# Wider weight blocks, undivided rooms and another last turn in a mixture-of-experts stage

## The chip, the core and the metric

The kernel runs on one core of a Trainium2 chip. The metric is the device time of one execution in microseconds (us). A core has five engines that each work through an own list of instructions: TensorE (PE; the load of a matmul's stationary tile is listed as PEld), VectorE (DVE), ScalarE (ACT), GpSimd (POOL) and SyncE (SP). SP issues nearly all transfers (DMAs) here; sixteen DMA engines that all queues share carry them out.

## The reference

Two layers work on 256 latent and 256 context tokens of width 1024. A layer modulates its input, projects it, runs 8 heads of windowed attention beside 8 heads of a chunked state-space scan (SSD), projects both back and normalises; then a feed-forward part follows, dense in layer 0 and a mixture of experts in layer 1:

```python
def _moe(h, router, wg, wu, wd):
    top_v, top_i = lax.top_k((h @ router).astype(jnp.float32), TOP_K)      # 2 of 8
    gates = jax.nn.softmax(top_v, axis=-1)
    combine = jnp.sum(jax.nn.one_hot(top_i, N_EXPERTS) * gates[..., None], axis=-2)
    for e in range(N_EXPERTS):
        out = out + combine[..., e:e + 1] * _swiglu(h, wg[e], wu[e], wd[e])
```

`_swiglu` is (silu(h Wg) * (h Wu)) Wd with Wg, Wu of 1024 x 3584 and Wd of 3584 x 1024, all float32: 44.04 MB for an expert, 352.3 MB for eight, read once in each execution. Only latent tokens reach the experts.

## The kernel before

**The experts (`jobs`, L1340).** The experts are ranked by how many tokens chose them, and each rank has a fixed number of slots for tokens (32, 64, 96 or 192). Seven turns run in the rank order 0, 4, 2, 3, 5, 7, 6, with 32, 64, 96, 64, 64, 32 and 64 slots. Rank 1, with 192 slots (three tiles of 64), is the side expert, worked off in seven pieces between blocks of the turns. A turn cuts the 3584 hidden columns into blocks (`main`: 1024, 1024, 1024, 512); the side expert's pieces are 512 wide (`thin`). A step of one block loads gate and up weights and multiplies the gathered tokens with them (`gate_up`, in two halves), transposes the hidden values of the step before (`flip`), forms silu(gate)*up (`act`), and multiplies the hidden values of the step before with that block's rows of Wd (`down`). After an expert's last block its result is scattered back to the tokens (`evac`, `scatter`). A matmul has the tokens (64 or 32 columns) as its stationary tile and up to 512 weight columns as the moving one, so a tile of 32 slots costs PE half of what one of 64 costs.

**The rooms.** Every weight transfer of an expert is one call of `moe_raw` (L1268): 1 MB goes into the next of 15 rooms, which are taken in strict rotation and reused when the matmuls on their old contents are done. One row of a block that is contiguous in memory is one packet for each partition: 4 KB for 1024 columns, 2 KB for 512. A tile of Wd takes two neighbouring rows a partition, an 8 KB packet. Five of the 15 rooms are pairs of two 512 KB buffers: one in `accl`, and four made of `whi` and `wlo` of the pool `sp`. Into these a load goes as two transfers, a row of Wd at a time (4 KB packets).

**The pool `sp` earlier.** `whi` and `wlo` have four buffers each. Weight splitting (`split_unit`, L117, which makes a high and a low part of a float32 weight for three matmuls) takes one of both. In the mixers the decay matrices of the scan (`E`, L770: one of 512 KB for each 128 tokens and each of two head groups, read back through SP from `cscr`) take `wlo`, and the transposed attention weights (`pT`, L900) take `whi`.

**The order.** PE's list in the experts' stage is the order of the code. In the mixers attention, scan and the modulation (`wm`, 2 MB loads of w_mod and their matmuls `mod`) are woven together, and a planner places instructions; SP issues in the order in which the planner meets them, and an SP instruction that waits for its room holds all that stand behind it. POOL multiplies E (L775), builds W (L779, L782), the scan's scaled inputs xe (L722) and more, in its own order.

**The end.** The last block of the last turn closes the kernel: `gate_up`, `act`, `flip`, its rows of Wd, `evac`, the scatter straight into four `fin` banks that already hold the residual (`add_acc`), layer norm, and the output.

Of the kernel before, what the change touches and what calls it, by code (L numbers as in the profile page):

```python
# [18 lines left out]
P = 128  # L19
D = 1024  # L20
# [49 lines left out]
class Build:  # L70
# [44 lines left out]
    def split_unit(self, src, shape, nm="u"):  # L115

        nc = self.nc  # L117
        self.uid += 1
        hi = self.sp.tile(shape, F32R, tag="whi", name=f"{nm}h{self.uid}")
        lo = self.sp.tile(shape, F32R, tag="wlo", name=f"{nm}l{self.uid}")  # L120
        with self.tc.issue_after(self.hold.pop(0).ins) if self.hold else ExitStack():
            nc.scalar.activation(hi, src, AF.Copy)  # L122
        self.nsplit += 1
        if self.pool_share and self.nsplit % self.pool_share == 0:
            self.last_pooled = nc.gpsimd.tensor_tensor(lo, src, hi, op=OP.subtract)
        else:
            nc.vector.tensor_tensor(lo, src, hi, op=OP.subtract)  # L127
        return hi, lo
# [371 lines left out]
    def steps_dt(self, l, m, pp, dtt, at, lv):  # L500
# [5 lines left out]
        wd = self.sp.tile([P, NK, 32], F32R, tag="whi", name=f"wd{l}")  # L506
# [207 lines left out]
    def ssd(self, l, wk, lv, dtt, mix, tts):  # L714
# [45 lines left out]
        for tt in tts:  # L760
# [4 lines left out]
            for g in range(2):  # L765
# [4 lines left out]
                E = self.sp.tile([P, 2, 4, P], F32, tag="wlo", name=f"E{l}{tt}{g}")  # L770
# [54 lines left out]
    def attention(self, l, wk, qT, kT, v, mix, tts, q0):  # L825
# [60 lines left out]
        for n in range(len(items) + 1):  # L886
# [56 lines left out]
    def last_norm(self, xs):  # L943
# [3 lines left out]
        out = [self.sp.tile([P, D], F32, tag="whi", name=f"fin{self.uid}{i}") for i in range(2)]  # L947
# [320 lines left out]
    def moe_raw(self, src, nm, paired=False):  # L1268

        self.uid += 1  # L1270
# [4 lines left out]
        if isinstance(pool, list):  # L1275
            halves = []
            for i, (p, tag) in enumerate(pool):
                t = p.tile([P, D], F32, tag=tag, name=f"{nm}{self.uid}{i}").rearrange("p (k f) -> p k f", f=f)
                self.nc.sync.dma_start(t, rows[:, i * n // 2:(i + 1) * n // 2, :])
                halves.append(t)  # L1280
            return halves
        if pool is None:
            self.odd ^= 1
            t = self.first_raw[:, self.odd, :].rearrange("p (k f) -> p k f", f=f)
        else:
            t = pool.tile([P, n, f], F32, tag="mraw", name=f"{nm}{self.uid}")
        self.nc.sync.dma_start(t, rows)
        return [t[:, :n // 2, :], t[:, n // 2:, :]]
# [62 lines left out]
    def jobs(self, M, todo, J0=None, side=None, finish=None):  # L1351
# [7 lines left out]
        main = [(0, 1024), (1024, 1024), (2048, 1024), (3072, 512)]  # L1359
        thin = [(f, 512) for f in range(0, FE, 512)]  # L1360

# [5 lines left out]
        def banks(J, w):  # L1367

            return [[self.bank("gu") for _ in range(w // 512 if s == 64 else 1)] for s in J["tiles"]]

        def gate_up(J, blk, os, part):
            c0, w = blk
            kn = 2048 // w
            for r in range(part * NK // kn // 2, (part + 1) * NK // kn // 2):
                gr, ur = [self.moe_raw(weights(a[n][0], J["e"], r * kn * P, (r + 1) * kn * P, c0, c0 + w), "mg")
                          for n in ("moe_w_gate", "moe_w_up")]
                at = lambda m, kk: m[kk // (kn // 2)][:, kk % (kn // 2), :]
                for q, s in enumerate(J["tiles"]):
                    for kk in range(kn):
                        k = r * kn + kk  # L1380
                        g, u = at(gr, kk), at(ur, kk)
                        x = J["xe"][:, k, q * 64:q * 64 + s]
                        if s == 64:
                            for b, o in enumerate(os[q]):
                                cs = slice(b * 512, (b + 1) * 512)
                                self.beside(o, x, [g[:, cs], u[:, cs]], k == 0, k == NK - 1)
                        else:
                            hs = [slice(b * w // 2, (b + 1) * w // 2) for b in range(2)]
                            self.beside(os[q][0], x, [m[:, h] for m in (g, u) for h in hs], k == 0, k == NK - 1)
                for _ in range(kn):  # L1390
                    self.tick()

        def act(J, blk, os):

            hs, n = [], 0
            for s, two in zip(J["tiles"], os):
                w = 512 if s == 64 else blk[1] // 2
                for o in two:
                    if n % 2 == 0 or w < 512:
                        self.uid += 1  # L1400
                        t = pj.tile([P, 512], F32, tag="h", bufs=2, name=f"h{J['nm']}{self.uid}")
                        hs.append((t, w, []))
                        n = 0
                    h = t[n * 64:n * 64 + 64, :w]
                    nc.scalar.activation(h, o[:64, :w], AF.Silu)  # L1405
                    nc.vector.tensor_tensor(h, h, o[64:, :w], op=OP.mult)  # L1406
                    hs[-1][2].append(n)
                    n += 1
            return hs

        def flip(J, blk, hs):
# [14 lines left out]
            for s in J["tiles"]:  # L1426
                if s == 64:
                    hT = [flipped.pop(0) for _ in range(blk[1] // 512)]
                    out.append(lambda t, odd, hT=hT: hT[t // 2][:, t % 2 * 2 + odd, :])
                else:  # L1430
                    hT, m = flipped.pop(0), blk[1] // 512
                    out.append(lambda t, odd, hT=hT, m=m: hT[:, t % m * 2 + odd, t // m * 32:t // m * 32 + 32])
# [6 lines left out]
        def parts(s, rd):  # L1439
            w = D * s // P  # L1440
            return [rd[:, 0, c:c + w] for c in range(0, D, w)]

        def down(J, c, blk, hT):
            last = c == len(main) - 1
            if J["side"]:
                os = [self.bank("ys") for _ in hT]
            elif c == 0:
                os = J["y"] = [self.bank("y") for _ in hT]
            else:
                os = J["y"]  # L1450
            nt = blk[1] // 256
            for t in range(nt):
                rd = rows(J, blk, t)
                for s, o, x in zip(J["tiles"], os, hT):
                    for odd in range(2):
                        self.beside(o, x(t, odd), parts(s, rd[odd]), t + odd == 0 and (J["side"] or c == 0),
                                    t == nt - 1 and odd == 1 and (J["side"] or last))
            if not J["side"]:
                return
            for y, o in zip(J["ys"], os):  # L1460
                if c == 0:
                    nc.scalar.activation(y, o, AF.Copy)
                else:
                    nc.vector.tensor_tensor(y, y, o, op=OP.add)
# [74 lines left out]
        after = [(0, 1), (0, 2), (3, 3), (4, 3), (5, 0), (5, 2), (6, 0)]  # L1539
        steps = []  # L1540
        for n in range(len(todo)):
            for c in range(len(main)):
                steps.append((n, c))
                if (n, c) in after and side is not None:
                    steps.append(("side", after.index((n, c))))
# [10 lines left out]
        for n, c in steps + [(None, None)]:  # L1556
            if n is not None:
                need(n)
                blk = (thin if n == "side" else main)[c]
# [3 lines left out]
                if todo and (n, c) == (0, 1):  # L1563
                    fill("side", self.slots(J["side"], M, *side, f"s{self.uid}_", True))
                if n == 0 and c == 2:
                    fill("close", M["close"]())
                if n != "side" and c == 2 and n + 1 < len(todo):
                    fill(n + 1, self.slots(J[n + 1], M, *todo[n + 1], f"t{n + 1}_{self.uid}_"))
                os = banks(J[n], blk[1])
# [4 lines left out]
            if n is not None:  # L1574
                gate_up(J[n], blk, os, 1)
# [316 lines left out]
```

## Time and profile before

| | |
|---|---|
| median of 3 runs | 1830.56 us (1828.31 to 1832.91) |
| profiled execution | 1831.6 us, of which the span of its instructions is 1829.8 |
| mean granted clock of PE | 0.973 |
| busy share of the span | PE 95%, DVE 39%, ACT 26%, POOL 11% |
| traffic | 499.27 MB in 176000 packets |
| experts' stage | first weight transfer issued at 914.5 us, first matmul at about 974 us, last matmul of Wd ends at 1812.6 us |

The profile page cuts the span into 40 slices of 45.7 us; a digit is the busy share in tenths. The DMA share is the mean over 16 DMA engines of the time that their packets took; packets of neighbouring transfers overlap a little, so it can stand over 1. An instruction's time in the timeline is a group's first start and the length of the run of that group.

### The profile page before, as it was taken

The page shows a single profiled execution, that of the slowest core. Times are in us where ns is not written, and L with a number is a line of the kernel's source. Part 1 is how long each engine was busy: PE and PEld are TensorE (multiplying, and loading weights), DVE is VectorE, ACT ScalarE, POOL GpSimd, SP SyncE. Part 2 cuts the span into 40 slices and gives each one's busy share as a digit, 9 for nine tenths or more (in the row PEclk, how much of TensorE's full clock was granted, in tenths as well). Part 3 has the DMA queues.
Part 4 walks back from the last instruction along what each step waited for, and adds up shares of the span by engine and source line. Part 5 has one row for each costly group of instructions (what it writes and reads, how often), then busy time and mean ns, then how long its engine had stood idle before and what let it go on. Part 6 is the DMA issues. An engine that isn't in the chain of part 4 may idle for free.

```text
span 1829.8 us, 25533 instructions
## 1 busy us (share of the span) xinstructions
PE 1734.6 (95%) x10236; PEld 1037.4 (57%) x10236; DVE 712.8 (39%) x1232; ACT 476.2 (26%) x856; POOL 203.3 (11%) x202
## 2 busy tenths in 40 slices
PE   6999998999999999999899999999999999989996
PEld 4788446798988899887465343323333343333332
DVE  3356585772443368768675011101021110110122
ACT  1333454353222235545342110101011110000011
POOL 2000650230000041501412000000000000000000
PEclk8999999999999999999998999999999999999998
DMA  9533985131223212254879999999999999999994
GB/s 330 185 128 122 318 282 166 70 115 70 91 93 138 92 51 95 68 193 148 305 293 357 411 412 413 414 414 412 416 418 405 414 411 412 411 411 410 412 410 199
DMA packets 176000, 499.27 MB, mean 273 GB/s; under 512 B 32616, under 2 KB 43424, under 8 KB 161344
## 3 DMA queue, kind: packets, MB, share of 16 engines
q1 hardware_dynamic: 174848, 495.76, 70.7%
q8 instruction: 82, 1.34, 0.3%
q10 hardware_dynamic: 608, 1.58, 0.3%
q0 software_dynamic: 416, 0.21, 0.1%
q14 instruction: 46, 0.38, 0.1%
HBM read 496.37 MB, written 4.30 MB: 274 GB/s over the span
## 4 chain that ended last, share of the span: by engine, by line
PE 84%; DMA 7%; DVE 5%; ACT 1%; POOL 1%; issue 1%; SPq 0%; DVEq 0%; ACTq 0%; POOLq 0%
PE gu L1349 24%; PE y L1349 8%; PE fm L460 7%; PE fm L459 7%; PE fm L461 7%; PE ys L1349 4%; DMA mg<-in_moe_w_up_dram 3%; PE tm L459 3%; PE tm L460 3%; PE tm L461 3%; DMA wm<-in_w_mod_dram 2%; PE fo L461 2%; PE fo L460 2%; PE fo L459 2%; PE xe L1319 2%; PE hT L1419 1%
## 5 line engine op out<-in xcount | busy, mean ns | idle before, releaser
L460 PE MATMUL fm<-mlo,uh 128*128 128x512 f32 (+1 forms) x768 | 265.7, 347 | 8.9 <-DVE mlo L395 8.9
L459 PE MATMUL fm<-mhi,uh 128*128 128x512 f32 (+1 forms) x768 | 265.1, 348 | 6.7 <-ACT uh L122 4.3
L461 PE MATMUL fm<-mhi,ul 128*128 128x512 f32 (+1 forms) x768 | 264.3, 346 | 0.0
L460 PEld LDWEIGHTS fm<-mlo,uh 128*128 128x128 f32 x768 | 147.4, 192 | 29.4 <-DVE mlo L395 12.0
L459 PEld LDWEIGHTS fm<-mhi,uh 128*128 128x128 f32 x768 | 146.6, 192 | 27.0 <-ACT uh L122 4.5
L1406 DVE TENSOR_TENSOR ht<-ht,gu 64x512 f32<-64x512 f32 (+1 forms) x47 | 31.6, 673 | 327.8 <-ACT ht L1405 327.7
L461 PEld LDWEIGHTS fm<-mhi,ul 128*128 128x128 f32 x768 | 147.1, 192 | 18.4 <-DVE ul L127 0.8
L1349 PE MATMUL y<-md,hht 128*32 128x256 f32 (+1 forms) x1048 | 149.4, 495 | 1.7 <-DMA md<-in_moe_w_down_dram 1.7
L1349 PE MATMUL gu<-mg,xes__8731 128*64 128x512 f32 x600 | 141.6, 603 | 2.1 <-DMA mg<-in_moe_w_up_dram 1.2
L931 POOL TENSOR_TENSOR mv<-mv,mhalf 128x1 f32<-128x1 f32 x12 | 8.5, 722 | 941.9 <-DVE mv L930 941.6
L1349 PEld LDWEIGHTS y<-md,hht 128*32 128x32 f32 (+1 forms) x1048 | 50.7, 125 | 99.4 <-issue 82.8
L459 PE MATMUL fo<-uh,hh 128*128 128x256 f32 (+1 forms) x336 | 95.3, 286 | 0.0
L460 PE MATMUL fo<-ul,hh 128*128 128x256 f32 (+1 forms) x336 | 95.0, 285 | 0.0
L1423 ACT ACTIVATE hht<-hT 128x512 f32<-128x512 f32 (+2 forms) x32 | 15.0, 473 | 306.4 <-PE hT L1419 306.4
L1349 PEld LDWEIGHTS gu<-mg,xes__8731 128*64 128x64 f32 x600 | 44.7, 139 | 85.5 <-issue 78.9
L461 PE MATMUL fo<-uh,hl 128*128 128x256 f32 (+1 forms) x336 | 92.5, 285 | 0.0
L1406 DVE TENSOR_TENSOR hs<-hs,gu 64x512 f32<-64x512 f32 x21 | 14.5, 690 | 177.4 <-ACT hs L1405 177.4
L1349 PE MATMUL gu<-mg,xet__9610 128*64 128x512 f32 (+2 forms) x416 | 72.4, 565 | 2.1 <-DMA mg<-in_moe_w_up_dram 1.5
L460 PEld LDWEIGHTS fo<-ul,hh 128*128 128x128 f32 x336 | 63.3, 188 | 0.7
L459 PEld LDWEIGHTS fo<-uh,hh 128*128 128x128 f32 x336 | 63.0, 188 | 0.8
L461 PEld LDWEIGHTS fo<-uh,hl 128*128 128x128 f32 x336 | 62.0, 188 | 0.7
L1349 PE MATMUL ys<-md,hhs 128*64 128x512 f32 x264 | 59.3, 605 | 0.0
(443 smaller groups left out, 2860.4 us busy)
## 6 DMA issues: line engine op xcount, KB each, us to landing
mg<-in_moe_w_up_dram SPq DMA_DIRECT2D x64, 1024.0 KB
mg<-in_moe_w_gate_dram SPq DMA_DIRECT2D x61, 1024.0 KB
md<-in_moe_w_down_dram SPq DMA_DIRECT2D x55, 1024.0 KB
wm<-in_w_mod_dram SPq DMA_DIRECT2D x20, 2048.0 KB
md<-in_moe_w_down_dram SPq DMA_DIRECT2D x78, 512.0 KB
mg<-in_moe_w_gate_dram SPq DMA_DIRECT2D x72, 512.0 KB
mg<-in_moe_w_up_dram SPq DMA_DIRECT2D x70, 512.0 KB
mraw<-in_moe_w_down_dram SPq DMA_DIRECT2D x18, 1024.0 KB
```

The source lines that it names most:

```text
L459: nc.tensor.matmul(ps, ah, bh, start=first and i == 0, stop=False)
L460: nc.tensor.matmul(ps, ah, bl, start=False, stop=False)
L461: nc.tensor.matmul(ps, al, bh, start=False, stop=last and i == n - 1)
L931: self.last_pow = nc.gpsimd.tensor_tensor(mv[:, 2:3], mv[:, 2:3], self.mhalf[:, 0:1], op=OP.pow)
L1319: nc.tensor.matmul(tp[:, m * W:(m + 1) * W], M["xn"][i][:, j * P:(j + 1) * P], pick[i][:, :, 0:W // n], start=(i == 0), stop=(i == 1))
L1349: self.last_mm = self.nc.tensor.matmul(o[n * g:n * g + n, :w.shape[1]], x, w, start=first, stop=last)
L1406: nc.vector.tensor_tensor(h, h, o[64:, :w], op=OP.mult)
L1419: self.last_flip = nc.tensor.transpose(tp[:, jj * m:(jj + 1) * m], h[:m, c0:c0 + 255:2], self.ident[:m, :m])
L1423: nc.scalar.activation(t[:, :k, :m], tp[:, :k * m].rearrange("p (j s) -> p j s", j=k), AF.Copy)
```

## The change

Three things change in the experts, and one in the pool `sp`.

The pool `sp` has one tag `w` with four contiguous buffers of 1 MB in place of `whi` and `wlo`. A split weight takes one (both parts), E takes one for both head groups of 128 tokens, pT one for both heads of a pair. As a room such a buffer is filled by one transfer. The `accl` room stays a pair.

Turns with at most 64 slots run in blocks of 2048 and 1536 columns, a 128-row slice of gate or of up being one transfer (8 KB or 6 KB a partition, 1 MB or 768 KB). The turn of 96 slots and the last turn keep the four old blocks. The rank order becomes 0, 4, 2, 3, 5, 6, 7: the last turn has 32 slots and not 64. The pieces of the side expert stand behind other blocks, two of them in the first and two in the last turn, where there were two and one.

In a step, the late scatter and the preparation of the next expert move ahead of the second half of `gate_up`. The side expert's `down` issues both transfers of Wd rows first. At the end, the `fin` banks are taken after `act` and `flip`.

```diff
@@ split_unit, L117
-        hi = self.sp.tile(shape, F32R, tag="whi", name=f"{nm}h{self.uid}")
-        lo = self.sp.tile(shape, F32R, tag="wlo", name=f"{nm}l{self.uid}")
+        t = self.sp.tile([P, 2, D], F32R, tag="w", name=f"{nm}{self.uid}")
+        hi, lo = [t[:, i, :shape[1] * shape[2]].rearrange("p (a b) -> p a b", a=shape[1]) for i in range(2)]
...
@@ ssd, L770
-                E = self.sp.tile([P, 2, 4, P], F32, tag="wlo", name=f"E{l}{tt}{g}")
+                if g == 0:
+                    E2 = self.sp.tile([P, 2, D], F32, tag="w", name=f"E{l}{tt}")
+                E = E2[:, g].rearrange("p (r h t) -> p r h t", r=2, h=4)
...
@@ attention, L899
-                    if i == 0:
-                        pTs[hh] = self.sp.tile([P, 4, 256], F32, tag="whi", name=f"pT{l}{pair[0]}{h0 + hh}")
+                    if i == 0 and hh == 0:
+                        t = self.sp.tile([P, 2, D], F32, tag="w", name=f"pT{l}{pair[0]}{h0}")
+                        pTs = {n: t[:, n].rearrange("p (k q) -> p k q", k=4) for n in range(2)}
...
@@ moe_raw, L1275
             for i, (p, tag) in enumerate(pool):
-                t = p.tile([P, D], F32, tag=tag, name=f"{nm}{self.uid}{i}").rearrange("p (k f) -> p k f", f=f)
-                self.nc.sync.dma_start(t, rows[:, i * n // 2:(i + 1) * n // 2, :])
+                part = rows[:, i * n // 2:(i + 1) * n // 2, :] if n > 1 else rows[:, :, i * D:min(f, (i + 1) * D)]
...
+        elif isinstance(pool, tuple):
+            t = pool[0].tile([P, 2, D], F32, tag=pool[1], name=f"{nm}{self.uid}").rearrange("p a b -> p (a b)")
...
@@ jobs, L1359
-        main = [(0, 1024), (1024, 1024), (2048, 1024), (3072, 512)]
+
+        wide, mid = [(0, 2048), (2048, 1536)], [(0, 1024), (1024, 1024), (2048, 1024), (3072, 512)]
         thin = [(f, 512) for f in range(0, FE, 512)]
+        turns = [mid if t[2] > 64 or n == 6 else wide for n, t in enumerate(todo)]
+        blocks = lambda n: thin if n == "side" else turns[n]
...
-            kn = 2048 // w
+            kn = max(1, 2048 // w) if w != 1536 else 1
...
@@ down, L1439
             if J["side"]:
-                os = [self.bank("ys") for _ in hT]
...
+                rds = [rows(J, blk, t) for t in range(nt)]
+                for y, s, x in zip(J["ys"], J["tiles"], hT):
+                    o = self.bank("ys")
...
@@ the steps, L1539
-        after = [(0, 1), (0, 2), (3, 3), (4, 3), (5, 0), (5, 2), (6, 0)]
+        after = [(0, 0), (0, 1), (3, 1), (4, 1), (5, 1), (6, 0), (6, 1)]
...
             if prev is not None:
                 pn, pc, pb, h = prev
                 hT = flip(J[pn], pb, h)
+            if late is not None:
+                need("close")
+                scatter(J[late])
+                late = None
             if n is not None:
...
                 gate_up(J[n], blk, os, 1)
                 if finish and (n, c) == steps[-1]:
                     break
                 h = act(J[n], blk, os)
-            if late is not None:
-                need("close")
-                scatter(J[late])
-                late = None
...
@@ the end of jobs, L1594
+        rds = [rows(J, blk, t) for t in range(blk[1] // 256)]
+        h = act(J, blk, os)
+        hT = flip(J, blk, h)[0]
+        s = J["tiles"][0]
         fin = [[self.bank("fin") for _ in range(2)] for _ in range(2)]
...
@@ body, L1836
-                              [(self.sp, "whi"), (self.sp, "wlo")]]
+                              (self.sp, "w")]
...
-                    ranks = [0, 4, 2, 3, 5, 7, 6]
+                    ranks = [0, 4, 2, 3, 5, 6, 7]
                     self.jobs(M, [(turn[t], p, {0: 32, 2: 96, 7: 32}.get(p, 64), bt) for t, p in enumerate(ranks)], J0,
```

What SP issues in the mixer of layer 0, before and after. `wm` are the 2 MB loads of w_mod, `bias` the attention's biases, `wo` the two loads of the output projection's weights.

```order
29 L771 DMA E_1675<-cscr_106 128x2x512
30 L771 DMA E_1747<-cscr_106 128x2x512
31 L771 DMA E_1826<-cscr_106 128x2x512
32 L771 DMA E_1891<-cscr_106 128x2x512
33 L445 DMA bias_1943<-rscr_108 64x6x64 x4
...
47 L771 DMA E_2291<-cscr_106 128x2x512
48 L261 DMA wm_2233<-in_w_mod_dram 128x2x2048
49 L445 DMA bias_2243<-rscr_108 64x6x64 x4
50 L451 DMA wo_2563<-in_w_out_dram 128x8x512
51 L451 DMA wo_2693<-in_w_out_dram 128x8x512
52 L445 DMA bias_2370<-rscr_108 64x6x64 x4
```

```order
29 L445 DMA bias_1913<-rscr_108 64x6x64 x4
...
35 L261 DMA wm_1843<-in_w_mod_dram 128x2x2048
36 L773 DMA E_1649<-cscr_106 128x2x512 x2
37 L261 DMA wm_1873<-in_w_mod_dram 128x2x2048
...
44 L445 DMA bias_2210<-rscr_108 64x6x64 x4
45 L451 DMA wo_2527<-in_w_out_dram 128x8x512
46 L451 DMA wo_2653<-in_w_out_dram 128x8x512
47 L773 DMA E_2179<-cscr_106 128x2x512 x2
48 L445 DMA bias_2335<-rscr_108 64x6x64 x4
```

Four E of two token tiles stood ahead of the biases and of five of the `wm`; the first two now stand behind four more `wm`, and the last two behind both `wo` instead of ahead of them.

What PE does at the end, from the rows of Wd of the last block but one: `y` the products with Wd, `hT` the transposes of `flip`, `fin` the residual's banks.

```order
5922 L1349 MATMUL y_12403<-mraw_8213,hht_1298_1430_12696 64x512 x8
5923 L1349 MATMUL y_12403<-md_12722,hht_1298_1430_12696 64x512 x4
5924 L1349 MATMUL y_12403<-md_12728,hht_1298_1430_12696 64x512 x4
5925 L1419 MATMUL hT_12745<-cA,ht_1298_1443_12742 128x64 x4
5926 L1601 MATMUL fin_12734<-res_2531,cA 128x512
5927 L1601 MATMUL fin_12735<-res_2531,cA 128x512
5928 L1349 MATMUL y_12403<-md_12738,hht_1298_1445_12750 64x512 x4
5929 L1349 MATMUL y_12403<-md_12740,hht_1298_1445_12750 64x512 x4
```

```order
5793 L1361 MATMUL y_11917<-md_12375,hht_1303_1443_12299 32x256 x8
5794 L1361 MATMUL y_11917<-md_12385,hht_1303_1443_12299 32x256 x8
5795 L1361 MATMUL y_11917<-md_12395,hht_1303_1443_12299 32x256 x8
5796 L1438 MATMUL hT_12414<-cA,ht_1303_1456_12411 128x64 x2
5797 L1632 MATMUL fin_12419<-res_2495,cA 128x512
5798 L1632 MATMUL fin_12420<-res_2495,cA 128x512
5799 L1361 MATMUL y_11917<-md_12405,hht_1303_1458_12417 32x256 x4
5800 L1361 MATMUL y_11917<-md_12407,hht_1303_1458_12417 32x256 x4
5801 L1361 MATMUL y_11917<-md_12409,hht_1303_1458_12417 32x256 x8
```

The order at the end is the same; the matmuls have 256 moving columns where they had 512, twice as many of them for a tile of Wd.

## Rows read from the trace of the kernel before

**Rows 1.** The page's 40 slices: PE, DMA and GB/s.

```profile
PE   6999998999999999999899999999999999989996
DMA  9533985131223212254879999999999999999994
GB/s 330 185 128 122 318 282 166 70 115 70 91 93 138 92 51 95 68 193 148 305 293 357 411 412 413 414 414 412 416 418 405 414 411 412 411 411 410 412 410 199
```

**Rows 2.** Busy us (x count) per stretch: PE, PEld, DVE, ACT, POOL; PEclk, DMA share, GB/s.

```profile
1000.00:1200.00 200.00, 192.43 (x1174) 74.74 (x1170) 26.30 (x62) 22.15 (x44) 0.00 (x0) 0.99 1.03 412
1200.00:1400.00 200.00, 195.42 (x1194) 69.80 (x1194) 30.24 (x60) 20.77 (x41) 0.00 (x0) 0.97 1.03 414
1400.00:1600.00 200.00, 196.80 (x974) 70.30 (x974) 26.36 (x45) 19.26 (x36) 0.00 (x0) 0.99 1.03 412
1600.00:1780.00 180.00, 172.65 (x1052) 63.54 (x1044) 26.07 (x43) 17.61 (x34) 0.00 (x0) 0.96 1.03 411
```

**Rows 3.** All transfers of three stretches: 1045 to 1050, 1105 to 1150, 1790 to 1795.

```profile
DMA packets 1033, 1.99 MB, mean 398 GB/s; under 512 B 62, under 2 KB 62, under 8 KB 1033
DMA packets 4893, 18.57 MB, mean 413 GB/s; under 512 B 364, under 2 KB 364, under 8 KB 4891
DMA packets 289, 2.12 MB, mean 424 GB/s; under 512 B 31, under 2 KB 31, under 8 KB 31
```

**Rows 4.** The page's transfers of Wd: count, KB of each.

```profile
md<-in_moe_w_down_dram SPq DMA_DIRECT2D x55, 1024.0 KB
md<-in_moe_w_down_dram SPq DMA_DIRECT2D x78, 512.0 KB
mraw<-in_moe_w_down_dram SPq DMA_DIRECT2D x18, 1024.0 KB
```

**Rows 5.** Transfers of the stretch 1802 to 1806.

```profile
DMA packets 173, 0.69 MB, mean 172 GB/s; under 512 B 23, under 2 KB 23, under 8 KB 155
```

**Rows 6.** Timeline of PE and DVE at the end: start, length, engine, line, operation, count.

```profile
1807.07 1.99 PE L1601 MATMUL fin<-res,cA 128*128 128x512 f32 x4
...
1808.99 3.65 PE L1349 MATMUL y<-md,hht 128*64 128x512 f32 x16
1812.57 1.99 PE L1601 MATMUL fin<-res,cA 128*128 128x512 f32 x4
1812.69 0.75 DVE L1477 SCALAR_TENSOR_TENSOR yst<-y,wst,g 128x512 f32<-128x512 f32 x1 [11.68 <-PE y L1349]
```

**Rows 7.** Timeline of PE in an expert of 32 slots.

```profile
1110.76 1.93 PE L1349 MATMUL y<-mraw,hht 128*32 128x256 f32 x32
```

**Rows 8.** Timeline of DVE after an expert of 32 slots.

```profile
1704.96 1.96 DVE L1482 SCALAR_TENSOR_TENSOR yst<-y,wst,g 32x256 f32<-32x256 f32 x4 [0.55 <-PE y L1349]
```

**Rows 9.** Chain of waits in layer 0's mixer: start, length, what.

```profile
187.92 11.93 DMA wm<-in_w_mod_dram
...
224.75 13.46 DMA wm<-in_w_mod_dram
...
277.05 0.85 PE yd L792 x8
...
285.55 0.62 DVE mix L820 x2
...
297.97 2.07 ACT mxh L986 x4
```

**Rows 10.** Timeline of SP in layer 0's mixer.

```profile
238.34 0.37 SPq L771 DMA_DIRECT2D E<-cscr  x1
...
250.71 16.30 SPq L451 DMA_DIRECT2D wo<-in_w_out_dram  x2
267.10 4.20 SPq L445 DMA_DIRECT2D bias<-rscr  x4
```

**Rows 11.** Timeline of POOL: the last E of layer 0.

```profile
257.81 1.89 POOL L775 TENSOR_TENSOR E<-E,cs 128x1024 f32<-128x1024 f32 x1
```

**Rows 12.** Chain of waits in layer 1's mixer.

```profile
853.29 8.78 DMA E<-cscr
...
869.84 2.04 POOL xe L722 x2
```

**Rows 13.** Timeline of POOL at the first E of layer 1.

```profile
862.21 3.78 POOL L775 TENSOR_TENSOR E<-E,cs 128x1024 f32<-128x1024 f32 x2 [11.50 <-DMA E<-cscr]
```

More of the change, by code (lines that the diff above doesn't have):

```diff
@@ L946, in last_norm @@
         self.uid += 1
-        out = [self.sp.tile([P, D], F32, tag="whi", name=f"fin{self.uid}{i}") for i in range(2)]
+        out = self.sp.tile([P, 2, D], F32, tag="w", name=f"fin{self.uid}")
+        out = [out[:, i] for i in range(2)]
         gl = self.mraw[0].tile([P, 2, D], F32, tag="mraw", name=f"gl{self.uid}")
@@ L1536, in need @@
                 self.tick()
-        after = [(0, 1), (0, 2), (3, 3), (4, 3), (5, 0), (5, 2), (6, 0)]
-        steps = []
+        after = [(0, 0), (0, 1), (3, 1), (4, 1), (5, 1), (6, 0), (6, 1)]
+        steps, ns = [], 0
         for n in range(len(todo)):
-            for c in range(len(main)):
+            for c in range(len(turns[n])):
                 steps.append((n, c))
-                if (n, c) in after and side is not None:
-                    steps.append(("side", after.index((n, c))))
+                for _ in range(after.count((n, c)) if side is not None else 0):
+                    steps.append(("side", ns))
+                    ns += 1
         if not todo:
@@ L1558, in jobs @@
                 need(n)
-                blk = (thin if n == "side" else main)[c]
+                J[n]["blocks"] = blocks(n)
+                blk = blocks(n)[c]
                 if n == "side" and c == 0:
@@ L1562, in jobs @@
                                   for q in range(len(J[n]["tiles"]))]
[L1563 to L1569, printed above, removed]
+                os = banks(J[n], blk)
                 gate_up(J[n], blk, os, 0)
@@ L1573, in jobs @@
                 hT = flip(J[pn], pb, h)
+            if late is not None:
+                need("close")
+                scatter(J[late])
+                late = None
             if n is not None:
+                if todo and (n, c) == (0, 0):
+                    fill("side", self.slots(J["side"], M, *side, f"s{self.uid}_", True))
+                if (n, c) == (0, 1):
+                    fill("close", M["close"]())
+                if n != "side" and c == len(blocks(n)) // 2 and n + 1 < len(todo):
+                    fill(n + 1, self.slots(J[n + 1], M, *todo[n + 1], f"t{n + 1}_{self.uid}_"))
                 gate_up(J[n], blk, os, 1)
@@ L1602, in add_acc @@
                                                     start=True, stop=False)
-        rds = [rows(J, blk, t) for t in range(blk[1] // 256)]
-        h = act(J, blk, os)
-        hT = flip(J, blk, h)[0]
-        s = J["tiles"][0]
         add_acc(0, self.last_flip)
@@ L1610, in jobs @@
             for odd in range(2):
-                self.beside(J["y"][0], hT(t, odd), parts(s, rd[odd]), False, t == len(rds) - 1 and odd == 1)
+                self.beside(J["y"][0], hT[t][odd], parts(s, rd, odd), False, t == len(rds) - 1 and odd == 1)
         add_acc(1, self.last_mm)
```

128 lines of the change are left out of this document (70 added, 58 removed).

## The prediction

> **What bounds the kernel now.** I read the page's slices first, then busy time by stretch, then the transfers of chosen stretches, then the end's timeline and the chain of waits in the two mixers.
>
> The slices fall into two parts [rows 1]: up to about 960 us PE is busy and the DMA engines mostly are not; from about 1000 to 1780 us both are, and the rate stays between 405 and 418 GB/s. The stretches decide between the two [rows 2]: from 1000 to 1780 us the DMA share is 1.03 in each, while PE adds up to 192.43 + 195.42 + 196.80 + 172.65 = 757.3 of 780 us. PE has 22.7 us of idle time left and the transfers none: the experts' stage is bound by transfers, with PE close behind. How fast a byte comes therefore sets the length of that stage, how far PE is behind at its end sets the rest, and what happens before 914 us shifts the start.
>
> **Packets: what removing them is worth.** Three stretches are each almost of one packet size [rows 3]. Without the packets under 512 B (semaphores) they hold 971 packets in 5 us (1.99 MB: 2 KB each), 4529 in 45 us (4 KB) and 258 in 5 us (8 KB). With 16 engines that is 16 x 5000 / 971 = 82.4 ns for 2 KB, 159.0 ns for 4 KB and 310.1 ns for 8 KB. Twice the bytes never cost twice the time: 2 x 82.4 - 159.0 = 5.8 ns and 2 x 159.0 - 310.1 = 7.9 ns are what a packet costs beside its bytes. For 6 KB I take the middle of 4 and 8 KB, 234.6 ns.
>
> Now the count. Before, each of seven turns brings 6144 packets of 4 KB and 2048 of 2 KB for gate and up, the side expert 14336 of 2 KB. Wd is 8 x 14 = 112 tiles: 73 came whole (128 packets of 8 KB), 39 as 78 halves (128 of 4 KB each) [rows 4]. Together 28672 of 2 KB, 52992 of 4 KB, 9344 of 8 KB: 91008. After, five turns have 2048 packets of 8 KB and 2048 of 6 KB; the 96-slot turn, the last and the side expert keep theirs; one transfer in 15 still falls into the divided room. That makes 19072 of 2 KB, 16256 of 4 KB, 9600 of 6 KB, 22912 of 8 KB: 67840, for the same 352.3 MB. In engine time: 28672 x 82.4 + 52992 x 159.0 + 9344 x 310.1 ns = 13.69 ms, over 16 engines 855.4 us; after 13.51 ms, 844.5 us. **The packets give -10.9 us.** By the two fixed costs alone, 23168 fewer packets give 23168 x 5.8 / 16 = 8.4 to 23168 x 7.9 / 16 = 11.4 us. The lower end is 0, should something other than packets hold the rate.
>
> The Trainium skill, page "DMA: Bandwidth & Descriptors", section "Why small descriptors are slow (HBM only)", puts a packet's fixed cost at about three cycles; with the 850 MHz of its table of specifications that is an estimate of 3.5 ns, by which this term would be -5 us and the time 1823. The rows measure 5.8 to 7.9 ns here, so I keep theirs.
>
> **PE's work in the turns.** The matmuls of the turns are the same ones, in larger lumps: a wide block of 64 slots takes four banks, and its `act` runs while PE multiplies the step before with its rows of Wd, as before. Nothing is added. PE's 22.7 us of slack are more than the 10.9 us that the transfers give up, so PE does not become the bound on the whole. A 1536-column transfer leaves a quarter of its room empty, so for a stretch the 15 rooms hold less ahead of PE (11.8 MB, 29 us at 412 GB/s, where 15.7 MB lasted 38). A piece of the side expert has three tiles of slots, so three times the matmuls of a turn for the same bytes, and PE falls behind there; three pieces now stand behind the neighbouring blocks (5, 1), (6, 0) and (6, 1), where they stood behind (5, 0), (5, 2) and (6, 0). I take 0; bounds 0 and +11 (the whole gain of the packets spent on full rooms). The scatter moved ahead of the second half of `gate_up` issues the same matmuls and DVE adds while transfers set the pace: 0, at worst the few us of one scatter in the last step, which is in the bounds of the next term.
>
> **The end.** The last 0.69 MB land between 1802 and 1806 us [rows 5], the last weights near 1805. PE has no wait there: `fin` at 1807.07, the last 16 matmuls of Wd at 1808.99 for 3.65 us, and DVE takes the result at 1812.69 [rows 6], some 7.5 us behind the data. A last turn of 32 slots halves this: 32 matmuls of that shape take 1.93 us [rows 7], so 16 take 0.97 instead of 3.65, -2.7, and the tiles just before shorten alike, another -1.8. The earliest that PE can be done is a microsecond after the data, at 1806.5, which is -6.1. Between -4.5 and -6.1 I take -5.2. Against it, DVE takes a 32-slot result in four pieces, 1.96 us [rows 8], instead of one of 0.75: +1.2. **The end gives -4.** Bounds -5 and 0.
>
> **The mixers.** Here only the order changes, and neither the old wait nor the new one has a row for its new place.
> Layer 0: the first two waits for `wm` on the chain are 11.93 and 13.46 us [rows 9]; the four E (2 MB) that stood ahead of these loads now go behind them, which at the 412 GB/s of the full queues is a gain of up to 5 us there. The last two E stood at 238.34 and were used by POOL from 257.81 [rows 10, 11], 19 us of slack; now SP reaches them only behind both `wo`, at 267.1 [rows 10]. With 5 us to land, two POOL passes of 1.9 us and the DVE steps up to the scan's last product `yd`, that product comes at about 281 instead of 277.05 [rows 9]. The scan's last rows were done at 286.17 and the mixer ended at 297.97 in the attention [rows 9], so the scan has 11.8 us to spare, and 4 are hidden. If the two `wo` or the room come later, they are not.
> Layer 1: the chain begins with 8.78 us for E, and POOL is idle for 11.50 us until it comes, with xe queued behind two E on POOL up to 869.84 [rows 12, 13]. After the change xe and W come first; that can give up to 11.5 us. But PE is full soon behind, with attention and modulation that do not wait for E, and the later E now stand behind more `wm` and biases. I take **+1 for both mixers together**, bounds -10 (layer 1's wait gone) and +22 (below).
>
> **The sum.** 1831.6 - 10.9 - 4 + 1 = 1817.7 for the profiled execution; that one is 1.0 over the median of the runs, so 1816.7. I forecast 1817.
>
> **Rivals.**
> (a) The packets buy nothing, since the rate is held elsewhere. For it: 2 KB and 8 KB lie only 6% apart. Against it: the three sizes order themselves, and the DMA share is full. Time: 1831.6 - 4 + 1 = 1828.6 profiled, 1827.6 as a median.
> (b) The mixers lose more than the experts gain: one buffer of four now serves split weights, E and pT, where each had four of its own. The place is the last E of layer 0, behind `wo`, in a room that pT and the split of `wo` also want. If it goes out only when attention frees one, say at 290, `yd` comes at 304, 27 us late, and the scan's last rows at 313 where the mixer ended at 298: +15, and with half of that in layer 1 +22. Time: 1831.6 - 14.9 + 22 = 1838.7. It is slower than before as soon as the mixers lose more than 15. For it: both `wo` already hold SP for 16.3 us [rows 10]. Against it: E only moves a few us past its use.
> (c) The mixers gain: E no longer ahead of xe, -9 in layer 1. Time 1807.
> (d) The rooms run out: PE behind by the side pieces, rooms three quarters full, transfers pause. The packets' gain is then spent in part or whole: 1820 to 1828. Against it: PE's slack [rows 2].
>
> **Chances.** The forecast 0.55 (its own range 1811 to 1823), (a) 0.10, (b) 0.13, (c) 0.12, (d) 0.10. What this kernel's measurement can tell from no change is about 0.3%, 5.5 us: below 1825 is faster, above 1836 slower. Faster: the forecast and (c), most of (d), a little of (a) and of the mild cases of (b), 0.80. Same: the rest of (a) and (d) and mild (b), 0.13. Slower: 0.07. The range that leaves out 2 in 10: 1806 (under (c)) to 1831 (over (a) and most of (d)).
>
> **What would show it.** Packets: 23000 fewer, and 417 GB/s where 412 stood, with a DMA share still at 1.03; a share that dips between 1000 and 1780 is (d), and the same GB/s with fewer packets is (a). End: the last product with Wd about 3 us after the last data. Mixers: the first experts' matmul within a few us of 974; later by over 10 us is (b), earlier by 7 is (c). The forecast is wrong if the first matmul moves by more than 10 us, or if the rate does not rise.

## The result and the profile after

The changed kernel takes 1810.62 us (median of 4 runs, 1809.29 to 1813.26), the kernel before 1830.47 beside it: a ratio of 0.9888, 95% interval 0.9873 to 0.9904, some 20 us faster. 1817 was forecast, with 1806 to 1831 as its range. The profiled execution took 1809.3 us, with a span of 1807.1 (before 1831.6 and 1829.8).

The experts' stage can be cut out of both traces with two marks: the first gather of tokens by PE (`xe<-pickt`), and the moment DVE takes the last turn's result (`yst`). The rows of a tile give the first and last start of a group behind the durations; first before, then after.

```profile
L1319 PE MATMUL xe<-pickt,xn x224: 274/276/423, 970.4 to 1628.8; 128*128 128x64 f32 x64, 128*128 128x32 f32 x32, 128*128 128x128 f32 x16
```

```profile
L1331 PE MATMUL xe<-pickt,xn x224: 275/275/476, 961.7 to 1608.3; 128*128 128x64 f32 x64, 128*128 128x32 f32 x32, 128*128 128x128 f32 x16
```

The stage starts 8.7 us earlier. The end, in the timeline of after:

```profile
1781.12 3.64 PE L1361 MATMUL y<-md,hht 128*32 128x256 f32 x64
...
1785.07 1.98 PE L1632 MATMUL fin<-res,cA 128*128 128x512 f32 x4
...
1786.99 1.07 PE L1361 MATMUL y<-md,hht 128*32 128x256 f32 x16
1788.24 1.07 PE L1361 MATMUL y<-md,hht 128*32 128x256 f32 x16 [0.18 <-DMA md<-in_moe_w_down_dram]
...
1789.38 1.96 DVE L1507 SCALAR_TENSOR_TENSOR yst<-y,wst,g 32x256 f32<-32x256 f32 x4 [7.17 <-PE y L1361]
```

Where PE ran without a wait to the end [rows 6], its last sixteen matmuls now wait 0.18 us for the last tile of Wd: PE has caught up with the data. The last packets of 8 KB, which are Wd's, end at 1803.9 before and at 1787.8 after, and PE's last product at 1812.6 and 1789.3: 8.8 us behind the data before, 1.6 after (read packet by packet from the traces; the packets of 4 KB that come later still are `gl`, the layer norm's two parameters). DVE's four pieces take 1.96 us, as rows 8 said. The products with Wd at 1781.12 stood in two groups before:

```profile
1799.48 3.60 PE L1349 MATMUL y<-mraw,hht 128*64 128x512 f32 x16
1802.92 3.60 PE L1349 MATMUL y<-md,hht 128*64 128x512 f32 x16
```

From the first gather to `yst` it is 842.3 us before and 827.7 after, -14.6, of which 7.4 lie ahead of the end of those last packets and 7.2 behind it; from `yst` to the end of the span 17.1 and 17.7, +0.6. With the start that makes -22.7, the difference of the spans.

In the stretch that rows 2 show, all transfers from 1000 to 1780 us, first of before, then of after:

```profile
DMA packets 90080, 321.36 MB, mean 412 GB/s; under 512 B 6548, under 2 KB 6548, under 8 KB 81967
```

```profile
DMA packets 68018, 323.70 MB, mean 415 GB/s; under 512 B 5588, under 2 KB 5588, under 8 KB 47781
```

And the table by stretch of after (busy us of PE, PEld, DVE, ACT, POOL; granted clock, DMA share, GB/s):

```profile
1000.00:1200.00 200.00, 193.13 (x1178) 74.05 (x1176) 26.05 (x57) 22.29 (x44) 0.00 (x0) 0.98 1.01 414
1200.00:1400.00 200.00, 196.96 (x1172) 71.22 (x1170) 28.11 (x54) 19.12 (x38) 0.00 (x0) 0.97 1.02 417
1400.00:1600.00 200.00, 198.49 (x930) 71.89 (x928) 27.08 (x48) 19.37 (x36) 0.00 (x0) 0.98 1.01 417
1600.00:1760.00 160.00, 159.19 (x936) 58.57 (x936) 19.20 (x31) 15.52 (x31) 0.00 (x0) 0.99 1.02 413
```

The rate is up by 2 to 5 GB/s with fewer packets, and the DMA share is 1.01 or 1.02 where it was 1.03. PE's idle time is down from 22.7 us of 780 to 12.2 of 760: it is close to its own bound.

### The profile page after: what moved, and what is told of

The parts are those of the page before. It is cut to its first block, busy times and chain, and to the rows that moved or that the text cites. A ratio compares the mean times of both kernels' runs of the same rounds, so it can differ in the third digit from the quotient of the medians.

```text
span 1807.1 us, 25197 instructions
## 1 busy us (share of the span) xinstructions
PE 1729.4 (96%) x10232; PEld 1037.5 (57%) x10232; DVE 710.9 (39%) x1232; ACT 474.1 (26%) x855; POOL 194.4 (11%) x202
## 4 chain that ended last, share of the span: by engine, by line
PE 84%; DVE 6%; DMA 5%; issue 2%; ACT 1%; POOL 1%; SPq 0%; DVEq 0%; ACTq 0%; POOLq 0%
PE gu L1361 24%; PE y L1361 8%; PE fm L460 7%; PE fm L459 7%; PE fm L461 7%; PE ys L1361 3%; PE tm L459 3%; PE tm L460 3%; PE tm L461 3%; PE fo L461 2%; PE fo L459 2%; PE fo L460 2%; DMA mg<-in_moe_w_gate_dram 2%; PE xe L1331 2%; PE mod L267 1%
## 5 line engine op out<-in xcount | busy, mean ns | idle before, releaser
L460 PE MATMUL fm<-mlo,u 128*128 128x512 f32 (+1 forms) x768 | 265.8, 347 | 8.6 <-DVE mlo L395 8.6
L459 PE MATMUL fm<-mhi,u 128*128 128x512 f32 (+1 forms) x768 | 263.9, 346 | 6.7 <-ACT u L122 4.3
L461 PE MATMUL fm<-mhi,u 128*128 128x512 f32 (+1 forms) x768 | 264.1, 346 | 0.0
L460 PEld LDWEIGHTS fm<-mlo,u 128*128 128x128 f32 x768 | 146.7, 191 | 29.5 <-DVE mlo L395 12.1
L459 PEld LDWEIGHTS fm<-mhi,u 128*128 128x128 f32 x768 | 146.1, 191 | 27.3 <-ACT u L122 4.6
L461 PEld LDWEIGHTS fm<-mhi,u 128*128 128x128 f32 x768 | 146.7, 192 | 18.4 <-DVE u L127 0.8
L1361 PE MATMUL y<-md,hht 128*32 128x256 f32 (+1 forms) x1064 | 139.9, 476 | 0.2 <-DMA md<-in_moe_w_down_dram 0.2
L1361 PE MATMUL gu<-mg,xes__8552 128*64 128x512 f32 x528 | 125.9, 593 | 0.0
L459 PE MATMUL fo<-u,hh 128*128 128x256 f32 (+1 forms) x336 | 94.9, 285 | 0.0
L460 PE MATMUL fo<-u,hh 128*128 128x256 f32 (+1 forms) x336 | 94.8, 285 | 0.0
L461 PE MATMUL fo<-u,hl 128*128 128x256 f32 (+1 forms) x336 | 92.6, 285 | 0.0
L460 PEld LDWEIGHTS fo<-u,hh 128*128 128x128 f32 x336 | 63.0, 188 | 0.8
L459 PEld LDWEIGHTS fo<-u,hh 128*128 128x128 f32 x336 | 62.9, 187 | 0.8
L461 PEld LDWEIGHTS fo<-u,hl 128*128 128x128 f32 x336 | 62.3, 188 | 0.7
```

The lines of the kernel that those rows point to most:

```text
L459: nc.tensor.matmul(ps, ah, bh, start=first and i == 0, stop=False)
L460: nc.tensor.matmul(ps, ah, bl, start=False, stop=False)
L461: nc.tensor.matmul(ps, al, bh, start=False, stop=last and i == n - 1)
L1361: self.last_mm = self.nc.tensor.matmul(o[n * g:n * g + n, :w.shape[1]], x, w, start=first, stop=last)
```

## The experiments

Each was timed against the kernel before on the same chip. The last three columns come from its profile: the start of the last projection matmul (`fm`), behind which layer 1's mixer begins; the first gather; and the time from there to the last turn's first `yst`. The last differs by 4.5 us between two kernels with the same experts' part (before and e9), so a single profile tells no less than that. Each profile is of one execution: those of e6 and e9 are of the slowest of their runs, that of e7 is of one 6 us faster than the median of its runs. e8 and e11 stand in the text.

| run | ratio to before, 95% interval | last `fm`, us | first gather, us | gather to `yst`, us |
|---|---|---|---|---|
| before | 1 | 862.4 | 970.4 | 842.3 |
| after | 0.9888 [0.9873, 0.9904] | 856.5 | 961.7 | 827.7 |
| e1 narrow blocks | 0.9917 [0.9896, 0.9938] | 857.6 | 959.2 | 834.1 |
| e2 heavy last | 1.0014 [0.9996, 1.0032] | 855.3 | 958.4 | 857.9 |
| e3 pool only | 0.9937 [0.9921, 0.9953] | 857.3 | 958.6 | 842.7 |
| e4 halves | 0.9941 [0.9921, 0.9962] | 862.1 | 970.5 | 829.2 |
| e5 rows of 4 KB | 0.9916 [0.9898, 0.9934] | 856.9 | 958.8 | 832.5 |
| e6 POOL's E held | 1.0027 [1.0014, 1.0040] | 865.0 | 975.4 | 846.5 |
| e7 heavy last, side earlier | 0.9956 [0.9939, 0.9972] | 854.6 | 956.3 | 840.2 |
| e9 SP's E later | 0.9953 [0.9941, 0.9966] | 854.5 | 961.3 | 846.8 |
| e10 side spread | 1.0045 [1.0028, 1.0061] | 857.3 | 961.1 | 857.3 |
| e12 three blocks last | 0.9907 [0.9891, 0.9922] | 858.4 | 964.0 | 834.3 |

**e3 and e4: the pool, alone and taken back.** e3 is the kernel before with the tag `w` everywhere; e4 the changed kernel with `whi` and `wlo` everywhere.

```diff
+        t = self.sp.tile([P, 2, D], F32R, tag="w", name=f"{nm}{self.uid}")    # e3, split_unit; E, pT, rooms likewise
-                              (self.sp, "w")]                                  # e4, body; E, pT, split_unit likewise
+                              [(self.sp, "whi"), (self.sp, "wlo")]]
```

> The kernel before with only the pool of four contiguous buffers for split weights, E, pT and rooms; blocks, rank order, step order as before. 87296 packets instead of 91008. Theory M (the mixers' new order alone moves the start of the experts by 8 to 9 us): first experts' gather at 961 to 963 instead of 970, plus 1.5 to 2 us by packets: 1819 to 1821. Rival (the early start is eaten up, since the transfers do not begin earlier or the end waits elsewhere): 1827 to 1830.

> The changed kernel with the two old tags of half buffers in place of the contiguous ones: E, pT and split weights as before, four rooms of 15 filled by two transfers (77056 packets, 473 transfers). Theories M and P: start as before (970), packets between: 1819 to 1823. Rival (the contiguous buffers matter for nothing but the number of transfers): 1811 to 1814.

e3 starts the experts at 958.6, 11.8 us early, and is 0.63% faster, 11.5 us; its stage is as long as before. e4 starts at 970.5 as before. So the earlier start is the pool's work alone. Taking it back costs 0.53% (e4 against after), near the 0.63% that it gives by itself. The 3712 packets fewer of e3 (some 1 us) do not show.

**e6 and e9: which queue.** e6 keeps SP's order of before and only puts POOL's use of E behind the xe. e9 keeps pools and buffers of before and only moves SP's transfers of E behind the newest w_mod load and the newest biases.

```diff
+                with self.tc.issue_after(self.last_xe.ins):                    # e6, around POOL's L775
+                with self.tc.issue_after(self.last_load.ins), (self.tc.issue_after(self.last_bias.ins) if hasattr(self, "last_bias") else ExitStack()):   # e9, around SP's L771
```

> The kernel before with one edge more: POOL's subtraction in E (L775) is placed behind the last scaled input xe in POOL's list, in both mixers; rooms and SP's transfers of E stay as they were, ahead of the biases and the w_mod loads. Theory M1 (POOL's 11.5 us wait for E with xe behind it made the start late): first experts' gather at 959 to 963, time 1819 to 1823. Rival M2 (SP's place of the E transfers, ahead of the w_mod loads, made it late): start at 968 to 971, 1829 to 1832.

> The kernel before, its pools and buffers untouched, with SP's transfers of E placed behind the newest w_mod load and the newest biases by two edges of order; in layer 1 the eight biases and three w_mod loads now go ahead of the first E. Theory M2 (SP's order made the experts start late): first experts' gather at 959 to 964, time 1819 to 1824. Rival M3 (it was the number of buffers or the single room of a split weight, not the order): start at 968 to 972, 1828 to 1832.

e6 does what it says on POOL: in layer 1, W and xe come first, at 865.34, and E at 887.86. It gains nothing and is 0.27% slower: layer 1's mixer begins 2.6 us later than before, and the experts 5.0. The 11.50 us for which POOL waits in rows 13 were not to be had: with E out of the way POOL waits just as long, for PE's last `fm`. POOL at that place in e6, then in after:

```profile
865.34 3.03 POOL L780 TENSOR_TENSOR W<-cA,dt 128x512 f32<-128x512 f32 x3 [12.04 <-PE fm L461]
```

```profile
856.82 3.04 POOL L781 TENSOR_TENSOR W<-cA,dt 128x512 f32<-128x512 f32 x3 [11.87 <-PE fm L461]
```

The first xe of e6 comes at 868.33, 3.3 us behind the start of the last `fm`, where it came 7.4 behind before [rows 12]: some 4 us, which e6 has lost again when the experts start. e6 holds E back in both mixers, so a loss at E's later use may hide a gain in it.

e9 starts the experts at 961.3, as early as after, with the buffers of before, and is 0.47% faster, 8.6 us. SP's order makes that gain. In the changed kernel E's transfers stand later too; that the four shared buffers bring this about through the planner is a reading that no run takes apart.

Where the time goes is read between the marks. Of e9's 9.1 us, 7.9 are there when layer 1's mixer begins; of after's 8.7, 5.9. In these two most of it is layer 0's. Over the eight kernels of the table with the new pool, 4.0 to 7.8 us are there at that mark, and 2.4 to 6.7 more come behind it, in layer 1 (in e3, the pool alone, 5.1 and 6.7). Layer 0's mixer and what follows up to the dense part, from 180 to 400 us (columns as above), of before:

```profile
180.00:200.00 20.00, 16.07 (x90) 6.90 (x92) 9.33 (x8) 9.31 (x25) 18.00 (x13) 0.99 0.97 265
...
180.00:400.00 220.00, 197.47 (x1184) 135.87 (x1183) 152.72 (x250) 105.80 (x238) 86.96 (x80) 0.96 0.54 184
```

Of after:

```profile
180.00:200.00 20.00, 19.16 (x112) 8.88 (x111) 6.43 (x9) 10.89 (x34) 12.62 (x12) 1.00 0.63 190
...
180.00:400.00 220.00, 199.37 (x1238) 140.07 (x1237) 155.03 (x254) 108.24 (x241) 81.44 (x78) 0.98 0.55 195
```

Of e9:

```profile
180.00:200.00 20.00, 19.87 (x116) 9.37 (x114) 5.93 (x8) 11.48 (x35) 12.35 (x12) 1.00 0.55 173
...
180.00:400.00 220.00, 202.12 (x1252) 142.54 (x1251) 149.31 (x255) 109.34 (x243) 82.44 (x78) 0.98 0.55 198
```

Of e5 (described below):

```profile
180.00:400.00 220.00, 203.09 (x1235) 143.04 (x1234) 155.01 (x254) 108.17 (x241) 81.92 (x78) 0.96 0.55 194
```

With the four E first, the DMA engines and POOL are full from 180 to 200 us and PE idles 3.9 us; with the biases first it idles 0.8 (after) and 0.1 (e9). Over the 220 us PE idles 22.5 us before, 20.6 after and 17.9 in e9. The granted clock, a mean of stretches at its full and at its half level, is 0.96 before and 0.98 in both others, by estimate worth some 4 us: 220 x 0.02. The two parts overlap, since what PE does in the stretches between is not the same work, but they are of the size of the 6 to 8 us. The clock is not needed for such a gain: e5 has the new pool and 0.96 as before, idles 16.9 us, and begins layer 1's mixer 5.5 us early. What is common to all is the earlier work of PE; how much of it is the clock's stays open. The waits for `wm` on the chain, by which the prediction priced this part, are not the measure: after has one of 9.18 us where before had two [rows 9], but e9 has two of 13.96 and 13.27, and gains more.

In layer 1, from the last `fm` to the first gather, it is 108.0 us before, 108.4 in e4, 106.8 in e9, and 101.3 to 105.6 in the kernels of the table with the new pool. In after it is 105.2. What the pool gives there beyond SP's order stays open.

**e1 and e5: packets.** e1 gives all turns the narrow blocks; e5 lays one row of Wd on a partition at a time, with the same transfers, rooms and matmuls.

```diff
-        turns = [mid if t[2] > 64 or n == 6 else wide for n, t in enumerate(todo)]
+        turns = [mid for t in todo]                                            # e1, and after = [(0, 1), (0, 3), (3, 3), ...]
-                                "md", True)
+                                "md")                                          # e5, rows; flip takes h[:m, jj*P:jj*P + P]
```

> The changed kernel, but every turn in the four old blocks (1024, 1024, 1024, 512), the side pieces behind the same columns; rooms, step order and the light last turn stay. 87296 packets instead of 67840. Theory P (packets set the pace of the experts' stage, 5.8 to 7.9 ns each): +7 to +9 us, so 1818 to 1820, first experts' matmul as in the changed kernel, rate back to about 412 GB/s. Rival (the gain of the stage lies in rooms, step order or places of the side pieces): 1810 to 1812.

> The changed kernel with the rows of Wd laid one to a partition and not two neighbouring ones, so that each of its transfers is two packets of 4 KB a partition; transfers, rooms, matmuls and their order stay, 13440 packets more (81280). Theory P with 5.8 to 7.9 ns a packet: +4.9 to +6.6 us, 1815.5 to 1817.2, rate 413 GB/s in the wide turns instead of 419. Rival (the rate does not hang on packets from 4 KB up): within 1 us of the changed kernel.

e1 is 0.29% over after, 5.3 us for 19456 packets, or 4.4 ns each with 16 engines; e5 0.28%, 5.1 us for 13440, 6.1 ns. Between their profiles it is 6.4 and 4.8 us. With the interval of after taken in, each of these differences is uncertain by over 4 us to either side, so neither run alone settles the price. The bytes moved from 1000 to 1780 us tell it more closely; e1, then e5 (after is shown above):

```profile
DMA packets 85017, 321.61 MB, mean 412 GB/s; under 512 B 5217, under 2 KB 5217, under 8 KB 73057
DMA packets 80260, 322.16 MB, mean 413 GB/s; under 512 B 5567, under 2 KB 5567, under 8 KB 72661
```

They move 2.09 and 1.54 MB less than after, at 415 GB/s 5.0 and 3.7 us, for 17370 and 12263 packets more (without those under 512 B): 4.6 and 4.8 ns. All of this speaks for about 5 ns a packet, e5 above all, in which beside packet size only the columns that `flip` reads change. For the change's 23168 that is some 7 us.

**e2 and e7: which turn is last.** e2 has the old rank order, with the 64-slot turn last and all else as changed; e7 also moves the last three side pieces ahead by one place.

```diff
-                    ranks = [0, 4, 2, 3, 5, 6, 7]
+                    ranks = [0, 4, 2, 3, 5, 7, 6]                              # e2 and e7
-        after = [(0, 0), (0, 1), (3, 1), (4, 1), (5, 1), (6, 0), (6, 1)]
+        after = [(0, 0), (0, 1), (3, 1), (4, 1), (5, 0), (5, 1), (6, 0)]       # e7
```

> The changed kernel with the old rank order (the 32-slot turn of rank 7 sixth, in wide blocks, the 64-slot turn of rank 6 last, narrow). Same packets, same start. Theory E (PE ends later behind the last data with 64 slots): the last product with Wd 6 to 8 us behind the last data instead of 0 to 2, time +5 to +7, 1816 to 1818. Rival (the end follows the data, whoever is last): 1810 to 1812.

> The changed kernel with the heavy turn last (64 slots, narrow) as in e2, and the side pieces of the end moved ahead: behind (5,0), (5,1) and (6,0) instead of (5,1), (6,0) and (6,1). Theory S (in e2 PE was 26 us behind the last data since three side pieces, each with more PE time than transfer time, stood just before a heavy end): PE's last product with Wd 4 to 10 us behind the data, 1815 to 1820. Rival (a heavy last turn alone costs that): 1830 and more.

e2 is 23 us slower than after, four times what theory E said. Its last stretches (columns as above) and its end:

```profile
1780.00:1800.00 20.00, 18.99 (x96) 7.58 (x94) 9.43 (x14) 3.08 (x5) 0.00 (x0) 1.00 0.57 220
1800.00:1820.00 20.00, 19.54 (x84) 6.81 (x80) 3.83 (x7) 1.60 (x3) 0.00 (x0) 1.00 0.00 0
```

```profile
1799.63 3.65 PE L1361 MATMUL gu<-mg,xet__11472 128*64 128x512 f32 x16
1803.12 7.04 PE L1361 MATMUL y<-md,hht 128*64 128x512 f32 x32
...
1812.62 3.65 PE L1361 MATMUL y<-md,hht 128*64 128x512 f32 x16
```

From 1800 us on no weight is moved, and PE works on for 16 us, at a granted clock of 1.00, its full level. The experts' own weights are in earlier still: from 1790 on there are only the two loads of `gl` (1.07 MB, issued at 1793.84 and 1794.22), and no packet of Wd (the one packet over 8 KB is of 16 KB, a load of instructions). The transfers of e2 from 1790 to 1800 and of e7 from 1782 to 1790:

```profile
DMA packets 289, 1.07 MB, mean 107 GB/s; under 512 B 32, under 2 KB 32, under 8 KB 288
DMA packets 165, 0.58 MB, mean 72 GB/s; under 512 B 24, under 2 KB 24, under 8 KB 165
```

PE's last product ends at 1816.27, 26 us behind the weights. Three side pieces and a 64-slot turn ask more of PE than the transfers leave it. In e7 the pieces come earlier, and the last product ends at 1796.4 with the weights in by 1782: 14 us behind instead of 26, and 0.9956 instead of 1.0014. Theory S holds in its direction; 4 to 10 us behind and 1815 to 1820 were expected, and the median is 1822.2. The light turn at the end and the late side pieces belong together.

**e8, e10, e11, e12: the places of the side pieces.** e8 has the last turn wide and the list of e7; with no block after the last piece, the side expert's result is not scattered in it, so its time is short of that work. e10 moves one piece out of the first block and one out of the last turn; e11 adds last blocks of 2048, 1024, 512; e12 has these blocks and both last pieces behind (6,0).

```diff
+        turns = [mid if t[2] > 64 else wide for n, t in enumerate(todo)]       # e8
+        after = [(0, 1), (1, 0), (1, 1), (3, 1), (4, 1), (5, 1), (6, 0)]       # e10, e11
+        after = [(0, 0), (0, 1), (3, 1), (4, 1), (5, 1), (6, 0), (6, 0)]       # e12
```

> The changed kernel with the last turn wide too, and the side pieces behind (5,0), (5,1), (6,0): 63872 packets instead of 67840. Theory P: -1.4 to -2 us by packets, and the end as before, for six tiles of Wd come last instead of two and PE keeps up with them: 1808 to 1811. Rival (narrow blocks at the end shorten what PE does behind the last data): 1813 to 1817.

> The changed kernel with the side pieces behind (0,1), (1,0), (1,1), (3,1), (4,1), (5,1), (6,0) instead of (0,0), (0,1), (3,1), (4,1), (5,1), (6,0), (6,1): none in the first block, one fewer at the end. Theory S (side pieces make PE late; at 1000 to 1050 us the rooms were full and the rate fell to 395): rate 410 to 419 in 1000 to 1050, 2 to 3 us less, 1807 to 1809. Rival (PE is late in turn 1 instead): 1810 to 1813.

> As e10, and the last turn in blocks of 2048, 1024 and 512 instead of 1024, 1024, 1024, 512: 1920 packets less. At 5.5 ns a packet -0.7 us beside e10: 1806 to 1809. Rival (the larger first block brings the side's last piece and its scatter closer to the end): 1810 to 1814.

> The changed kernel with the last turn in blocks of 2048, 1024 and 512, and its two side pieces both behind the first of them; all other side pieces stay where the change has them. 1920 packets fewer. At the 5.5 ns that e1 and e5 gave: -0.7 us, and the end as in the changed kernel, 1808 to 1812. Rival (two pieces at once make PE late at the end, as three did in e2): over 1814.

e10 was to be better and is 28 us slower than after. Its stretches:

```profile
1000.00:1020.00 20.00, 13.81 (x133) 4.26 (x124) 1.03 (x2) 0.86 (x2) 0.00 (x0) 0.83 1.02 422
1020.00:1040.00 20.00, 15.15 (x88) 4.63 (x86) 0.00 (x0) 0.00 (x0) 0.00 (x0) 0.74 1.03 414
...
1200.00:1220.00 20.00, 20.00 (x96) 6.75 (x94) 3.51 (x5) 2.40 (x4) 0.00 (x0) 1.00 0.80 314
```

The same first stretch in after:

```profile
1000.00:1020.00 20.00, 20.00 (x160) 7.93 (x160) 2.07 (x3) 2.37 (x4) 0.00 (x0) 1.00 0.91 369
```

With no piece in the first block PE idles 11 us from 1000 to 1040, as the light first turn does not fill it, and the share of transfers stays full there, as theory S said. But that idle time does not come back: from 1200 to 1400 us PE is busy for 198.9 of 200 us and the transfers stall (rates of 336 and 371 GB/s in its two hundreds). Whether the idle first block costs this, or the three pieces close together at (0, 1), (1, 0) and (1, 1), was not taken apart. After pays about 2 us for a full set of rooms at 1000 to 1020 and keeps PE working. e11 does the same (1.0037). e8 (0.9915 [0.9898, 0.9932]) stalls at 1600 to 1700, where the share is 0.94 and PE is busy without a gap. e12 cannot be told from after and is rather slower: PE's last product ends at 1798.17, 8 us behind the last packets of Wd. All four came out slower than expected. No version beat the changed kernel.

## Why the prediction came out as it did

Step by step, in the order of the sum (us, forecast and found):

- **Packets, -10.9; found some -6 to -9.** The mechanism is right (e1, e5), the size probably too large. The term that was mis-sized is the price of a packet: 5.8 to 7.9 ns were read from stretches of 5 us, where one packet more or less at an edge of the 8 KB stretch is 1.2 ns; e1 and e5 give 4.4 and 6.1 by their ratios, which are too wide to exclude 5.8, and 4.6 and 4.8 by their bytes. The Trainium skill's three cycles ("DMA: Bandwidth & Descriptors", "Why small descriptors are slow (HBM only)"), 3.5 ns as an estimate, lie below all four, within the intervals of the ratios.
- **PE's work and the rooms, 0; found about +2 here.** The rate dips to 369 GB/s at 1000 to 1020 us, by estimate 2 us. With it the stretch up to the last packets of Wd is 7.4 us shorter, where -10.9 was forecast. The bound of +11 that was kept was too small for the mechanism: e2 and e10 show that other places of the side pieces cost 23 and 28 us. "PE's 22.7 us of slack are more than the 10.9 us that the transfers give up" counted the slack over the whole stage; it has to be there when the data come.
- **The end, -4; found some -7 (7.2 us less from the last packets of Wd to `yst`, 0.6 more behind it).** PE now waits for the last tile, as forecast, and DVE's +1.2 came. The sum had two slips that cancel in part: the last tiles take 32 of the narrower matmuls and not 16 (1.93 us by rows 7, not 0.97), and the tiles just before them shorten by some 3.5 us, from the two groups of before to the 3.64 us at 1781.12 of after, and not by 1.8. From e3 to e1, which have nearly the same start and the same packets, the ratio falls by 0.0020 (3.7 us, uncertain by over 4) and the stage by 8.6; PE's last product ends 11.3 us behind the last packets of Wd in e3 and 1.6 in e1. This step also holds the new places and the step order, which were not taken apart. That the light turn is worth far more with three side pieces at the end (e2) was not seen.
- **The mixers, +1; found -8.7 in the trace, -11.5 us by e3's ratio.** This is the term that failed, and its 9.7 us are more than the whole difference between 1817 and 1810.6. Rival (c) named the size, -9 in layer 1, with a chance of 0.12, and by the prediction's own sign ("earlier by 7 is (c)") it is what came; but the place is only partly layer 1: of the 8.7 us in this trace 5.9 are there before layer 1's mixer begins. The step "a gain of up to 5 us there" for layer 0 was right in kind and was then cancelled in the sum by costs that no row showed. The 11.50 us that POOL waits in layer 1 [rows 13] were taken as the most that could be gained there; e6 shows POOL waiting 12.04 us for PE's last `fm` without them.
- **Layer 0's last E behind `wo`, hidden; held.** SP issues it at 260.54, and the mixer's end moves from 297.97 [rows 9] to 295.42, forward and not back.
- Rival (a) falls with e1 and e5 together, (b) with every start of the new pool before 965, and (d) is true of the neighbours of this change.
- That 1817 lies within 7 us of 1810.6 is in part luck: the transfers gave some 3.5 us less than forecast, against the 9.7 us by which the mixers and the 2.6 by which the end gave more.

By ratios, taken in this order, the parts of the -1.12% are: pool -0.63% (e3), light turn with new places and step order -0.20% (e1 against e3), wide blocks -0.29% (after against e1). The last two are uncertain by over 0.2% each.

## What to carry to other kernels

Where a queue is in order, ask of a moved transfer what stands behind it there and which engine wants that first; the engine that waits longest in the chain need not be the one that costs time. Where two resources are both nearly full, an average slack says little; heavy pieces belong where the other work is light: in e10 idle time of the nearly full engine was not made up. A packet's fixed cost should be read from long stretches, or measured by one change that alters as little else as can be.

## What the hardware showed beyond that

Between 4 and 8 KB, at rates over 400 GB/s, packet size still counts: some 5 ns a packet (e1, e5). Short waits went with a lower granted clock in e10: it was 0.83 and 0.74, means of its full and its half level, in the two stretches in which PE was busy for 13.8 and 15.2 of 20 us, and 1.00 in the first of these stretches of after, where PE had no gap. In layer 0 a mean of 0.96 against 0.98 over 220 us goes with an earlier end by some 6 us in after, but e5 has nearly the same gain at 0.96.
